# Five written-out instruction orders replaced, in a fused fp32 decoder layer

## The chip, the core and the metric

The kernel runs on one core of one Trainium2 chip. The metric is the device time of one launch in microseconds (us). Of each program several executions are timed, and one more is recorded by the hardware profiler; "the profiled execution" is that one.

## The reference

One layer of a hybrid decoder on 2048 prompt tokens and 8 single decode tokens, width 1024, in fp32:

```
xn  = rmsnorm(x);  z = xn @ w_in            # 1024 -> 1792: conv branch, gate branch, q, k, v
rec = RG-LRU(causal_conv4(xr)) * gelu(gr)   # a per-token scan, 512 channels
att = banded attention, 8 heads of 64, 2 kv heads, window 128, learned sinks
h   = x + concat(rmsnorm(rec), rmsnorm(att)) @ w_out
y   = h + (silu(rmsnorm(h) @ w_gate) * (rmsnorm(h) @ w_up)) @ w_down     # 2816 wide
out = rmsnorm(y)                            # and the last k/v rows, conv and scan states
```

The decode tokens use given caches of k, v, conv input and scan state.

## The kernel before

**Products.** Channels lie on the 128 partitions, tokens along the free axis. Each fp32 product is three matmuls of a reduced fp32 form (fp32r): both operands are split into a high part and a low rest, and hi·hi, hi·lo and lo·hi are accumulated in PSUM. So each weight tile is loaded raw, cast on ACT (`split_raw`, L936) and its rest formed on POOL (L937); each activation is cast on ACT and its rest formed on DVE or POOL (L998/L999).

**First half, to about 660 us.** The tokens go through in four tiles of 520, 512, 512 and 512. For each tile: norm; the in-projection in 14 units of 128 outputs (`ip0_9_1` is tile 0, unit 9, second half of the columns), each 24 matmuls per accumulator; conv and scan; attention block by block; the norms of the two groups; the out-projection in 8 units (`op2_5_0` is tile 2, unit 5), 24 matmuls each; the residual sum (L1638, and L1686/L1687 for the last tile) and its store to `hs` (for the last tile on ACT's queue, L1688). An attention block has scores `s`, a mask and a scale on DVE (L1515, L1526), transposes `pt`, a cast `pth` of them on ACT (L1536) and the rest `ptl` on DVE (L1537), and the product `o` with v. `pt14_1_0` is block 14, kv group 1, first part. The tiles of weights in tile 0 are loaded raw (`raw_in0_9_0`, L931), split, and stored split to DRAM (L955); tiles 1 to 3 load the split form.

**Second half, the FFN.** The tokens go in three pairs of column halves (344+344, 342+342, 342+342), and for each pair over 11 pairs of hidden blocks. For gate and up (`g`, `u`), two column halves by two hidden blocks are formed by seven products instead of eight (Strassen's scheme in Winograd's form, `w_g2_0_6`: pair 2, block pair 0, product 6); their sums of weights are made in the first token pair and kept in DRAM (`split_g`, `split_u`), and loaded later (L1802); raw blocks come by L1790 (`ru`, `rg`). `mixed` in DRAM holds the sums of the normed activations; `n0_3_1` (L1082, L1090) is such a sum on its way there, `hn` (L1137 to L1139) its load and split. Down (`pd`, L2021; `pw` with 14 rounds, L2050) is plain in some block pairs and has seven products in others. A last norm ends the kernel.

**PSUM.** Accumulators of the projections come from a pool of three banks (`ps_acc`); `ps_s` has two, `ps_t`, `ps_o` and `ps_m` one each. A tile of a pool becomes free when the operation that evicts it has ended.

**What sets the order.** Each part of the work is a generator with planned times. What an engine executes, though, is fixed by `ORDER`, a dictionary of five strings, for PE (12043 instructions), DVE (2566), ACT (1815), POOL (795) and SP (1416, each a DMA issue). A string is a list of runs `name:n`: the next n instructions of the part named so. `order` and `order_engines` walk each string and tie each instruction to the one ahead of it:

```
for run in runs.split():
    key, _, at = run.partition("+")
    key, _, n = key.partition(":")
    for _ in range(int(n or 1)):
        r = todo[key].pop(int(at or 0))
        if last is not None:
            tc.add_manual_dep(r, last.name, no_sync, reason="issue order")
        last = r
```

Each engine works through its own string in order. What it must wait for from other engines comes from the data and the buffers. A DMA that stands on SP or ACT is issued when the queue reaches it.

Of the kernel before, what the change touches and what calls it, by code (L numbers as in the profile page):

```python
# [117 lines left out]
vt0_2 ip0_13_0:13 ip0_13_1:6 vt0_3 ip0_13_1:16 ip0_2_0 ip0_13_1 ip0_2_0 ip0_13_1 ip0_2_0:4 s0_0_0:2 ip0_2_0:2 s0_0_0
ip0_2_0 s0_0_0 s0_0_1 ip0_2_0:3 s0_0_1:2 ip0_2_0:3 g0_0_0_0 ip0_2_0:4 s0_0_1 ip0_2_0:4 ip0_2_1:4 s0_1_0 ip0_2_0
ip0_2_1 s0_1_1 s0_1_0:3 ip0_2_1:2 s0_1_1:3 ip0_2_1:2 g0_0_0_260 ip0_2_1:10 s1_0_0 ip0_2_1 s1_0_0:2 ip0_2_1:2 s1_0_0  # L120
ip0_2_1 pt0_0_1 ip0_2_1 pt0_0_1:3 ip0_5_0:2 s1_0_1:2 ip0_5_0:2 s1_0_1:2 ip0_5_0:4 g0_0_1_0 ip0_5_0:10 o0_0_0 ip0_5_0:6
s1_1_0 ip0_5_1:2 s1_1_0:3 ip0_5_1:6 g0_0_1_260 ip0_5_1:3 pt0_1_1:3 ip0_5_1:3 pt0_1_1 o0_0_0 ip0_5_1:2 s1_1_1 ip0_5_1:4
s1_1_1 ip0_5_1 s1_1_1:2 ip0_5_1 ip0_4_0 ip0_5_1:2 ip0_4_0:3 s2_0_0:2 ip0_4_0 s2_0_0 ip0_4_0 s2_0_0 ip0_4_0:4 o0_1_0
ip0_4_0:6 o0_1_0 pt1_0_0 ip0_4_0 pt1_0_0 ip0_4_0:2 pt1_0_0 ip0_4_0:2 pt1_0_0 s2_0_1:4 ip0_4_0 ip0_4_1:2 ip0_4_0
ip0_4_1:6 ip0_4_0 ip0_4_1:16 ip1_8_0:12 ip0_6_0 ip1_8_0:3 ip0_6_0:5 o1_0_0 ip0_6_0:4 pt1_0_1:2 ip0_6_0 ip1_8_0 pt1_0_1
ip0_6_0 o1_0_0 pt1_0_1 g0_3_0_0 ip0_6_0:12 ip0_6_1 ip1_8_0 ip0_6_1:8 ip1_8_0 ip0_6_1:3 s2_1_0 ip0_6_1:3 s2_1_0 ip1_8_0
ip0_6_1 s2_1_0:2 ip0_6_1:4 s2_1_1 ip0_6_1:3 s2_1_1:2 o1_0_1 ip0_6_1 s2_1_1 g0_3_0_260 ip1_8_0:2 pt1_1_0 ip1_8_0
pt1_1_0:2 ip1_8_0 pt1_1_0 ip1_8_0 ip1_9_0:2 o1_0_1 ip1_9_0:9 g0_3_1_0 ip1_9_0:7 ip0_7_0:2 ip1_9_0 ip0_7_0:3 ip1_9_0
ip0_7_0:4 ip1_9_0:3 pt1_1_1:2 o1_1_0 ip1_9_0 ip0_7_0 pt1_1_1:2 o1_1_0 ip0_7_0:4 g0_3_1_260 ip0_7_0:7 s3_0_0 ip0_7_0:3
# [2130 lines left out]
```

## Time and profile before

| | |
|---|---|
| runs | 2035.62 us median of 3 (2033.41, 2041.63, 2035.62) |
| profiled execution | 2035.2 us |
| its span | 2033.4 us |
| mean granted TensorE clock | 0.995 of full speed |
| DMA | 450.98 MB, mean 222 GB/s |

The span runs from the first to the last recorded instruction; the execution's own time has 1.8 us more around it. A line of the timeline gives start, duration, engine, code line, operation, output and inputs by the program's names, the count, and in brackets how long the engine had been idle and what it waited for. PE is TensorE's matmul, PEld its weight load, DVE VectorE, ACT ScalarE, POOL GpSimd, SPq and ACTq the DMA issues of SyncE and ScalarE.

### The profile page before, as it was taken

How to read it: one execution, taken by the hardware profiler on the slowest of the kernel's cores; microseconds unless marked ns; L12 is line 12 of the kernel's file. 1: busy time of each engine (PE TensorE's matmuls, PEld its weight loads, DVE VectorE, ACT ScalarE, POOL GpSimd, SP SyncE). 2: the span in 40 equal slices, each digit the busy share in tenths (PEclk: the TensorE clock that was granted, in tenths of full speed). 3: DMA queues.
4: the chain of work that ended last, by engine and by line, in shares of the span. 5: the costliest groups of instructions: out<-in, count | busy, mean ns of one | idle time of the engine just before them, and what ended most of it. 6: DMA issues, size and time to landing. Idle time of an engine off the chain costs nothing.

```text
span 2033.4 us, 34750 instructions
## 1 busy us (share of the span) xinstructions
PE 2004.7 (99%) x12273; PEld 1904.5 (94%) x12273; DVE 1472.9 (72%) x2694; ACT 955.0 (47%) x1960; POOL 906.8 (45%) x799
## 2 busy tenths in 40 slices
PE   9999999999999999999999999999999999999997
PEld 8988887888778999999999999999999999999997
DVE  6888986777886777765555777787767666776675
ACT  5776764654563543443344533343335433433443
POOL 4312451120132796676666645565557422322333
PEclk9999999999999999999999999999999999999999
DMA  9863675667688776764546687776668675555552
GB/s 338 297 215 127 225 273 182 210 197 223 206 288 272 285 245 208 240 212 168 184 172 224 229 282 242 261 240 214 228 209 290 204 236 196 182 197 199 195 173 101
DMA packets 208991, 450.98 MB, mean 222 GB/s; under 512 B 25232, under 2 KB 82720, under 8 KB 208800
## 3 DMA queue, kind: packets, MB, share of 16 engines
q1 hardware_dynamic: 205184, 445.73, 65.2%
q10 hardware_dynamic: 3632, 3.02, 0.5%
q8 instruction: 97, 1.59, 0.3%
q14 instruction: 78, 0.64, 0.1%
HBM read 335.89 MB, written 113.84 MB: 221 GB/s over the span
## 4 chain that ended last, share of the span: by engine, by line
PE 88%; DMA 6%; DVE 4%; issue 1%; ACT 1%; SPq 0%; DVEq 0%; ACTq 0%
PE ps_g L963 20%; PE ps_u L963 20%; PE ip L963 14%; PE pw L963 12%; PE pd L963 11%; PE op L963 5%; PE s L963 1%; DMA m<-mixed 1%; PE g L963 1%; PE pt L968 1%; PE o L963 1%; DMA mixed<-n 1%; DMA y<-hs 1%; DMA xs<-in_xT 0%; DMA hn<-mixed 0%
## 5 line engine op out<-in xcount | busy, mean ns | idle before, releaser
L963 PE MATMUL ps_g<-hn,w_g 128*128 128x342 f32 (+1 forms) x2772 | 546.0, 320 | 1.8 <-DMA w_g<-split_g 1.0
L963 PE MATMUL ps_u<-hn,w_u 128*128 128x342 f32 (+1 forms) x2772 | 529.8, 320 | 4.5 <-ACT c_u L1985 3.5
L963 PEld LDWEIGHTS ps_u<-hn,w_u 128*128 128x128 f32 x2772 | 455.0, 189 | 5.5 <-ACT c_u L1985 3.8
L963 PEld LDWEIGHTS ps_g<-hn,w_g 128*128 128x128 f32 x2772 | 456.6, 189 | 2.5 <-ACT w_d L1778 2.3
L963 PE MATMUL ip<-xn,w_in 128*128 128x512 f32 (+1 forms) x1680 | 367.3, 361 | 3.9 <-ACT w_in L936 2.7
L963 PEld LDWEIGHTS ip<-xn,w_in 128*128 128x128 f32 x1680 | 271.5, 190 | 49.4 <-issue 4.8
L2050 DVE TENSOR_TENSOR y<-y,pw 128x342 f32<-128x342 f32 x504 | 242.7, 506 | 94.8 <-PE pw L963 90.4
L963 PE MATMUL pd<-fh,w_d 128*128 128x344 f32 (+1 forms) x960 | 235.0, 320 | 0.0
L963 PE MATMUL op<-mix,w_out 128*128 128x512 f32 (+1 forms) x960 | 209.8, 362 | 0.3 <-DVE mix L999 0.3
L2021 DVE TENSOR_TENSOR y<-y,pd 128x344 f32<-128x344 f32 (+1 forms) x240 | 119.6, 509 | 103.3 <-PE pd L963 91.1
L963 PEld LDWEIGHTS op<-mix,w_out 128*128 128x128 f32 x960 | 157.6, 190 | 30.0 <-issue 6.1
L963 PE MATMUL pw<-fh,wd 128*128 128x342 f32 x576 | 167.5, 319 | 1.0 <-DVE y L2021 1.0
L963 PEld LDWEIGHTS pd<-fh,w_d 128*128 128x128 f32 x960 | 167.3, 188 | 0.0
L963 PE MATMUL pw<-t,wd 128*128 128x342 f32 x648 | 150.6, 319 | 0.0
L963 PE MATMUL pd<-fl,w_d 128*128 128x344 f32 (+1 forms) x480 | 147.6, 320 | 0.0
L1946 POOL TENSOR_TENSOR c_u<-c_u,c_g 128x342 f32<-128x342 f32 (+1 forms) x60 | 58.8, 980 | 180.2 <-DVE c_u L1964 144.5
L1964 DVE TENSOR_TENSOR c_u<-c_u,ps_u 128x342 f32<-128x342 f32 (+1 forms) x99 | 50.5, 510 | 122.1 <-PE ps_u L963 121.8
L1935 DVE TENSOR_TENSOR fl<-c_u,fh 128x342 fp32r<-128x342 f32 (+1 forms) x132 | 118.5, 909 | 15.3 <-ACT fh L1934 14.2
L1779 POOL TENSOR_TENSOR w_u<-ru,w_u 128x512 fp32r<-128x512 f32 x44 | 58.9, 1340 | 151.8 <-ACT w_u L1778 123.0
L1934 ACT CAST fh<-c_u 128x342 fp32r<-128x342 f32 (+1 forms) x132 | 62.1, 479 | 106.4 <-POOL c_u L1946 41.9
L963 PEld LDWEIGHTS pw<-t,wd 128*128 128x128 f32 x648 | 111.4, 189 | 0.0
L963 PEld LDWEIGHTS pw<-fh,wd 128*128 128x128 f32 x576 | 105.6, 189 | 1.3 <-DVE y L2021 1.3
(299 smaller groups left out, 3499.9 us busy)
## 6 DMA issues: line engine op xcount, KB each, us to landing
w_g<-split_g SPq DMA_DIRECT2D x88, 512.0 KB, 4.4
w_u<-split_u SPq DMA_DIRECT2D x88, 512.0 KB, 5.5
w_in<-split_w SPq DMA_DIRECT2D x84, 512.0 KB, 3.6
rg<-in_wgate SPq DMA_DIRECT2D x110, 256.0 KB, 3.1
ru<-in_wup SPq DMA_DIRECT2D x110, 256.0 KB, 3.3
w_out<-split_w SPq DMA_DIRECT2D x48, 512.0 KB, 4.8
split_g<-w_g SPq DMA_DIRECT2D x44, 512.0 KB, 2.8
split_u<-w_u SPq DMA_DIRECT2D x44, 512.0 KB, 2.9
```

The source lines that it names most:

```text
L963: r = nc.tensor.matmul(*args, **kw)
L968: r = nc.tensor.transpose(*args)
L1779: lo_eng.tensor_tensor(w[:, 1, :], src, w[:, 0, :].bitcast(F32), op=ALU.subtract)
L1934: nc.scalar.copy(hi, v)
L1935: nc.vector.tensor_tensor(lo, v, hi.bitcast(F32), ALU.subtract)
L1946: (nc.vector if p == NPAIR - 1 or src is not v else eng(E_MUL[2 * h + n])).tensor_tensor(v, src, g, op=ALU.mult)
L1964: nc.vector.tensor_tensor(o, a, b, op)
L2021: nc.vector.tensor_tensor(ys[gi, n, m], ys[gi, n, m], ps, ALU.add)
L2050: nc.vector.tensor_tensor(v, v, ps, ALU.add)
```

## The change

The five strings of `ORDER` are replaced. All other code is the same, and each string holds the same instructions as before, in another order. The PE string has 11089 runs instead of 4667, DVE 2094 instead of 1968, ACT 1492 instead of 1476, POOL 629 instead of 624, SP 1152 instead of 1127. On PE the median instruction stands 0.79 us of matmul work away from its old place, 95% less than 3.3 us, the farthest 26.6 us. As the strings are longer, all code behind them has line numbers 406 higher (L1537 becomes L1943). One place of the PE string, around the out-projection of tile 2 and attention block 14:

```
-op2_5_0:10 s15_1_0:3 op2_5_0:2 s15_1_1 op2_5_0 s15_1_1 s15_1_0 s15_1_1:2 o14_0_1 op2_5_0:4 o14_0_1 op2_5_0:6
-pt14_1_0:3 op2_5_0 op2_6_0 pt14_1_0 op2_6_0:22 op2_7_0 op2_6_0 op2_7_0:5 st_rc3 pt14_1_1:4 op2_7_0:5 o14_1_0 op2_7_0:3
...
+op2_5_0 op2_6_0 op2_5_0 op2_6_0 op2_5_0 op2_6_0 op2_5_0 op2_6_0 op2_5_0 op2_7_0 op2_5_0 op2_7_0 op2_5_0 op2_7_0
+op2_5_0:3 op2_6_0 op2_7_0 op2_6_0 op2_7_0 op2_6_0 op2_7_0 op2_6_0 pt14_1_1 op2_6_0 pt14_1_1 op2_6_0 pt14_1_1 op2_6_0
```

Three places on other engines follow. The first is SP, the loads at the start of the kernel. Here `raw_in0_u_i` is a raw half of unit u's weights of the in-projection, `xs0` a part of the x tile, `xt1` rows of the next tile, `cs`, `scv`, `gw` and `sh` constants and states, `split_w` the store of split weights, `out_skw` and `out_svw` copies of the k and v caches to outputs. Before:

```order
L1239 DMA cs_101<-in_cst 128x384
L1185 DMA gw_132<-in_gatew 128x1024
L1184 DMA scv_137<-in_sconv 128x96
L931 DMA raw_in0_12_1_185<-in_win 128x512
L955 DMA split_w_117<-w_in0_1_0_166 128x1024
L1186 DMA sh_138<-in_sh0 128x32
L931 DMA raw_in0_9_0_368<-in_win 128x512
L955 DMA split_w_117<-w_in0_12_0_171 128x1024
L1292 DMA xt1_0_1418<-in_xR 128x512
L1292 DMA xt1_1_1421<-in_xR 128x512
L1178 DMA out_skw<-in_ck 8x16256
L1179 DMA out_svw<-in_cv 8x16256
```

The next row there is `raw_in0_9_1`. After:

```order
L1655 DMA xs0_188<-in_xT 128x520
L1337 DMA raw_in0_12_1_185<-in_win 128x512
L1655 DMA xs0_188<-in_xT 128x520
L1337 DMA raw_in0_9_0_368<-in_win 128x512
L1590 DMA scv_137<-in_sconv 128x96
L1361 DMA split_w_117<-w_in0_12_0_171 128x1024
L1698 DMA xt1_0_1418<-in_xR 128x512
L1361 DMA split_w_117<-w_in0_1_0_166 128x1024
L1698 DMA xt1_1_1421<-in_xR 128x512
L1337 DMA raw_in0_9_1_374<-in_win 128x512
L1645 DMA cs_101<-in_cst 128x384
```

`raw_in0_12_1` and `raw_in0_9_0` stand among the x parts now, `raw_in0_9_1` ahead of `cs`; `out_skw`, `sh`, `gw` and `out_svw` stand later, in this order, with other loads between them.

The second is DVE, near the end of the first half (588 to 597 us in the profile before): the scan of tile 3 (`q23_1`, `rrec`), the scale of the probabilities of block 15 (`sc15`), the residual of tile 2 (`xres2_5`), a sum of normed activations for the FFN (`n0_3`), and the rest `ptl14_1_0` of the transposed probabilities of block 14. Before:

```order
L1376 SCALAR_TENSOR_TENSOR q23_1_5902<-ia3_3_5945,carry_135,ix3_3_5952 128x512
L1384 SCALAR_TENSOR_TENSOR rrec_144<-rrec_144,q23_1_5902 128x512 x2
L1526 TENSOR_SCALAR sc15_0_6723<-sc15_0_6723,mx15_0_6724 128x256 x2
L1638 TENSOR_TENSOR xres2_5_6137<-xres2_5_6137,op2_5_0_6188 128x512
L1082 SCALAR_TENSOR_TENSOR n0_3_1_5510<-n0_3_1_5510,vec_99,hb_0_1_5363 128x344
L1082 SCALAR_TENSOR_TENSOR n0_3_0_5513<-n0_3_0_5513,vec_99,hb_0_0_5356 128x344
L1090 TENSOR_TENSOR n0_3_1_5510<-n0_3_1_5510,n0_3_0_5513 128x344
L1537 TENSOR_TENSOR ptl14_1_0_6701<-pt14_1_0_6695,pth14_1_0_6700 128x512
```

After:

```order
L1782 SCALAR_TENSOR_TENSOR q23_1_5902<-ia3_3_5945,carry_135,ix3_3_5952 128x512
L1943 TENSOR_TENSOR ptl14_1_0_6701<-pt14_1_0_6695,pth14_1_0_6700 128x512
L1790 SCALAR_TENSOR_TENSOR rrec_144<-rrec_144,q23_1_5902 128x512
L1955 TENSOR_TENSOR ratt_145<-o14_0_6659,ratt_145 64x4x128
L2044 TENSOR_TENSOR xres2_5_6137<-xres2_5_6137,op2_5_0_6188 128x512
L1488 SCALAR_TENSOR_TENSOR n0_3_1_5510<-n0_3_1_5510,vec_99,hb_0_1_5363 128x344
L1488 SCALAR_TENSOR_TENSOR n0_3_0_5513<-n0_3_0_5513,vec_99,hb_0_0_5356 128x344
L1496 TENSOR_TENSOR n0_3_1_5510<-n0_3_1_5510,n0_3_0_5513 128x344
L1932 TENSOR_SCALAR sc15_0_6723<-sc15_0_6723,mx15_0_6724 128x256 x2
```

`ptl14_1_0` moved from behind the `n0_3` rows to right behind the scan, and the scale of block 15 moved behind them.

The third is SP at the start of the last token pair (about 1555 us): `hn2_*` are loads of its activations, `y2_0` loads from `hs`, `rg` and `ru` raw weight blocks, `w_g2_0_6` the gate weights of product 6. Before:

```order
L1790 DMA ru2_0_00_17775<-in_wup 128x512
L1137 DMA hn2_0_6_17545<-mixed_113 128x342
L1790 DMA rg2_1_00_17912<-in_wgate 128x512
L1137 DMA hn2_0_7_17549<-mixed_113 128x342 x2
L1790 DMA rg2_0_11_17805<-in_wgate 128x512
L1137 DMA hn2_1_0_17572<-mixed_113 128x342
L1137 DMA hn2_1_1_17576<-mixed_113 128x342 x2
L1774 DMA y2_0_18171<-hs_112 128x342 x2
L1802 DMA w_g2_0_6_17543<-split_g_114 128x1024
```

After:

```order
L1543 DMA hn2_0_7_17549<-mixed_113 128x342
L2196 DMA rg2_1_00_17912<-in_wgate 128x512
L2180 DMA y2_0_18171<-hs_112 128x342
L1543 DMA hn2_1_0_17572<-mixed_113 128x342
L1543 DMA hn2_0_7_17549<-mixed_113 128x342
L1543 DMA hn2_1_1_17576<-mixed_113 128x342
L2208 DMA w_g2_0_6_17543<-split_g_114 128x1024
L2180 DMA y2_0_18171<-hs_112 128x342
L1543 DMA hn2_1_2_17599<-mixed_113 128x342
L2196 DMA ru2_0_00_17775<-in_wup 128x512
L1543 DMA hn2_1_1_17576<-mixed_113 128x342
```

`w_g2_0_6` stands ahead of one of the two `y2_0` loads, of `ru2_0_00` and of the second `hn2_1_1` load now.

Three more moves: on PE the matmuls that use the gate weights `w_g1_0_6` (about 1112 us) and `w_g2_0_6` (about 1562 us) stand seven FFN matmuls later among the others; on DVE the operation for `fl1_4_01` (L1935, about 1330 us) stands 17 rows earlier; on ACT the load of an activation table (L1943, about 672 us) stands five rows earlier among its neighbours, the store of `xres3_4` to `hs` (L1688, about 674 us) behind it one row earlier, and the copy `c_u0_0_10` (L1985, about 680 us) still behind both.

More of the change, by code (lines that the diff above doesn't have):

```diff
@@ new lines @@
+op0_5_260 op0_6_0 op0_5_260 op0_6_260 op0_5_260 op0_6_260 op0_5_260 op0_6_0 op0_5_260 op0_6_0 op0_5_260 op0_6_0
+op0_5_260 g1_3_1_0 op0_5_260 op0_6_0 op0_6_260 op0_6_0 o6_0_0 op0_6_0 op0_5_260 op0_6_0 pt6_0_1 op0_6_0 pt6_0_1
+op0_6_0 op0_5_260 bc_x2_0 op0_6_0 op0_6_260 op0_6_0 pt6_0_1 op0_6_0 op0_6_260 op0_6_0 pt6_0_1 op0_6_0 op0_6_260
+op0_6_0 op0_6_260 op0_6_0 o6_0_0 op0_6_260 op0_7_0 op0_6_260 op0_7_0 op0_6_260 op0_7_0 op0_6_0 op0_6_260 op0_7_0
+op0_6_260 s7_1_0 op0_6_260 op0_6_0 op0_6_260 pt6_1_0 op0_6_260 o6_0_1 s7_1_0 op0_6_260 o6_0_1 op0_6_260 s7_1_0
@@ new lines @@
+d2_10_1_1 d2_10_2_1 d2_10_4_1 d2_10_2_1 d2_10_3_1 d2_10_2_1 d2_10_3_1 d2_10_4_1 d2_10_3_1 d2_10_4_1 d2_10_3_1
+d2_10_5_1 d2_10_6_1 d2_10_3_1 d2_10_6_1 d2_10_3_1 d2_10_5_1 d2_10_4_1 d2_10_7_1 d2_10_6_1 d2_10_5_1 d2_10_4_1
+d2_10_7_1 d2_10_5_1 d2_10_7_1 d2_10_5_1 d2_10_7_1 d2_10_5_1 d2_10_6_1 d2_10_7_1 d2_10_6_1 d2_10_7_1 d2_10_6_1
+d2_10_0_0 d2_10_2_0 d2_10_0_0 d2_10_2_0 d2_10_0_0 d2_10_1_0 d2_10_0_0 d2_10_3_0 d2_10_0_0:2 d2_10_1_0 d2_10_2_0
+d2_10_1_0:4 d2_10_2_0 d2_10_3_0 st_f2_1:3 d2_10_2_0 d2_10_3_0 d2_10_5_0 d2_10_3_0 d2_10_6_0 d2_10_5_0 d2_10_3_0
@@ L572 @@
[L572 to L574 removed]
+pre pre+2 pre+3 pre+3 pre+1 pre+1 pre pro+3 pro pro+2 pro pro+15 pro:5 x0:6 x0+1 x0+2 x0+3 x0+4 x0:5 pro:3 r01+3 r01+4
+x0 pro:6 r01 q02 r01 pro:2 pro+1 pro k0 v0+1 v0 q02 r01:2 k0 r01 k0 r00:2 k0+2 k0+1 k0 k1+1 k1+1 r03:2 r01+1 q01 r01
@@ L686 @@
+pu2.6:3 wd2.6 wg2.7 wd2.6 wu2.7 pu2.7:2 wd2.7 pu2.7:3 wd2.7 wg2.8 wd2.7 wu2.8 pu2.8:2 wd2.8 pu2.8:3 wd2.8 wg2.9 wd2.8
+wu2.9 pu2.9:2 wd2.9 pu2.9:3 wd2.9 wg2.10 wd2.9 wd2.10 wu2.10 wd2.10 wd2.10+1 wd2.10 f21:3 f20:8
 """,
     "SP": """
-x0:9 x0+1 x0+1 x0+1 pro+1 pro x0 r01 pro v0 q02 xs1:2 cache:2 v0+1 r01 k0 q02 k0+1 v0 r00 v0 xs1:2 r00+1 k0 r03 k0
-r03+1 r00 xs1:2 q01 r00 q01+1 r03 q00 r03 xs1:2 q00+1 q01 q03 q01 q03+1 x1 q00 x1 r02 q00 r02+1 q03 x1 g01 q03 x1
-g01+1 r02 g00 r02 x1:2 g00+1 g01:2 g02 x1 g00 k1 g02+1 g03 x1 k1 g00 g02 g03+1 xs2 v1 g02 v1 xs2:2 o00 cache g03 o00+1
@@ L741 @@
[L741 to L745 removed]
+x0+1 x0:4 x0+2 x0 x0+1 x0 x0+1 x0:2 v0 pro q02 xs1 r01 xs1 v0+1 x0 k0 r01 xs1 v0 k0+1 r00 q02 r00+1 xs1 cache pro+1 k0
@@ new lines @@
+r03 v0 r03+1 xs1 pro k0 q01 r00+1 xs1 q01+1 r00 r03 q00 xs1:2 q00+1 cache q03 q01 r03 x1 q03+1 x1 q01 r02 q00:2 r02+1
+x1 g01 x1 q03:2 r02 g01+1 x1 g00 r02 x1 g00+1 g01 x1 g02 g01 g00 g02+1 x1 k1 g03 k1 xs2 g00 g02 g03+1 v1 g02 o00 v1
+xs2:2 cache g03 o00+1 q10 g03 o01 q10 q11 xs2 dec:2 q11 g10 xs2:3 g10 r10:2 xs2 o00+2 x2 q12:2 q13 x2 q13 r11:2 g11:2
+r12:2 g12:2 r13 o01+3 r13 g13:2 o01+1 o00 o02 o00 o02+1 o01 o03 o01 o03+1 o02 x2:2 o02 o04 o00 x2 o04+1 o03 o02 x2 o01
+o05 o03 x2 o03 x2 o02 o05+1 o04+2 o04 o06 o04 o06+1 o05 o03 o07 o05:2 o07+1 o06 o04 o06 wg0.0 o06 g20 o07 wg0.0 o07
@@ L746 @@
+wg2.9 wu2.8+4 wd2.8 wg2.9 wu2.8 wd2.8:3 wu2.8 wd2.8 wu2.8:2 wg2.9+4 wu2.9 wg2.9 wd2.8 wg2.9 wd2.8 wg2.9 wu2.9 wg2.9
+wd2.8 wg2.10 wu2.9+4 wd2.9 wg2.10 wd2.9+1 wu2.9 wd2.9:3 wu2.9:3 wu2.10 wg2.10+4 wg2.10 wd2.9 wg2.10 wd2.9 wg2.10:2
+wu2.10 wd2.9 wd2.10:2 wu2.10+4 wd2.10:2 wu2.10:4 f21:8 f20:4
 """,
```

1640 lines of the change are left out of this document (1013 added, 627 removed).

## The prediction

> **What bounds the kernel now.** I read the page first, then the busy time by stretches of the span, then the single instructions around each hole on TensorE.
>
> ```profile
> span 2033.4 us, 34750 instructions
> PE 2004.7 (99%) x12273; PEld 1904.5 (94%) x12273; DVE 1472.9 (72%) x2694; ACT 955.0 (47%) x1960; POOL 906.8 (45%) x799
> PE 88%; DMA 6%; DVE 4%; issue 1%; ACT 1%; SPq 0%; DVEq 0%; ACTq 0%
> ```
>
> TensorE is busy for 99% of the span, and the chain that ended last is TensorE for 88% of it. So order can win only where TensorE stands idle or runs at a lowered clock. The stretches show where; the columns are the stretch, its length, the busy time of PE, PEld, DVE, ACT and POOL with their counts, the granted clock, the DMA share and GB/s.
>
> ```profile
> 0.00:27.00 27.00, 22.09 (x149) 21.16 (x150) 15.77 (x33) 16.47 (x30) 10.22 (x16) 0.94 0.90 332
> 27.00:584.00 557.00, 556.17 (x3167) 473.40 (x3167) 453.31 (x968) 351.62 (x745) 143.84 (x162) 1.00 0.68 224
> 584.00:621.00 37.00, 32.27 (x151) 25.98 (x150) 29.21 (x57) 18.34 (x42) 12.53 (x11) 0.91 0.71 233
> 621.00:660.00 39.00, 38.74 (x183) 31.70 (x183) 24.58 (x37) 14.03 (x29) 12.43 (x9) 1.00 0.94 318
> 660.00:685.00 25.00, 21.35 (x119) 20.25 (x118) 18.33 (x27) 13.12 (x27) 16.44 (x13) 0.93 1.02 376
> 685.00:1203.00 518.00, 515.37 (x3289) 514.30 (x3288) 342.66 (x503) 217.29 (x433) 345.28 (x264) 1.00 0.63 215
> 1203.00:1564.00 361.00, 359.58 (x2286) 359.03 (x2285) 272.61 (x473) 142.37 (x288) 212.05 (x193) 1.00 0.71 237
> 1564.00:2010.00 446.00, 446.00 (x2848) 445.94 (x2847) 303.58 (x575) 173.76 (x354) 145.79 (x127) 1.00 0.59 195
> 2010.00:2033.40 23.40, 13.08 (x95) 12.71 (x93) 12.81 (x28) 8.00 (x16) 8.26 (x9) 0.83 0.36 121
> 605.71:609.12 3.41, 2.34 (x14) 1.73 (x14) 3.41 (x5) 1.67 (x4) 1.27 (x1) 1.00 0.94 296
> 609.12:615.95 6.83, 5.64 (x17) 4.39 (x17) 6.25 (x13) 4.10 (x8) 1.52 (x1) 0.50 0.53 156
> 677.39:680.80 3.41, 0.35 (x2) 0.35 (x3) 0.44 (x2) 0.84 (x3) 2.36 (x2) 1.00 1.04 409
> 680.80:684.21 3.41, 3.41 (x14) 3.41 (x13) 0.94 (x2) 2.15 (x5) 1.70 (x2) 0.50 1.04 413
> ```
>
> Length less PE busy gives the idle time: 4.91 at the start, 0.83, 4.73, 0.26, 3.65, 2.63, 1.42, 0.00, and 10.32 in the end, 28.75 us in all. The last four rows are windows inside the others. Two of them show a granted clock of 0.50, and of the 5.64 and 3.41 us that TensorE was busy in these, half is lost: 2.8 and 1.7 us. The rest is TensorE at its cadence, where the same multiset of instructions must take the same time, unless interleaving itself costs something.
>
> **The change part by part.** *Interleaved accumulators.* Where TensorE worked 10 or 24 matmuls on one accumulator, it now changes accumulator at almost every matmul. The trace has both forms in one place.
>
> ```profile
> 1107.94 3.45 PE L963 MATMUL ps_u<-hn,w_u 128*128 128x344 f32 x21
> 1112.16 0.55 PE L963 MATMUL ps_g<-hn,w_g 128*128 128x342 f32 x2 [0.78 <-ACT w_d L1778]
> 1112.56 0.32 PE L963 MATMUL ps_u<-hn,w_u 128*128 128x344 f32 x1
> 1112.71 0.32 PE L963 MATMUL ps_g<-hn,w_g 128*128 128x342 f32 x1
> ```
>
> Twenty-one in a row take 3.45 us, 0.156 us from start to start after taking off one 0.32 for the last one's length; alternating starts are 0.15 to 0.16 apart (1112.56, 1112.71). I cost the interleaving at nothing. The bounds are a hundredth of a microsecond either way, read off these starts.
>
> *Start.* SyncE issues its loads one after the other, and two matmul groups of the first token tile wait on weights.
>
> ```profile
> 14.26 0.83 SPq L1178 DMA_DIRECT2D out_skw<-in_ck  x1
> 15.15 0.67 SPq L1179 DMA_DIRECT2D out_svw<-in_cv  x1
> 15.93 0.37 SPq L931 DMA_DIRECT2D raw_in<-in_win  x1
> 24.58 0.62 ACT L936 CAST w_in<-raw_in 128x512 fp32r<-128x512 f32 x1 [2.76 <-DMA raw_in<-in_win]
> 15.29 8.32 PE L963 MATMUL ip<-xn,w_in 128*128 128x260 f32 x67 [0.44 <-ACT w_in L936]
> 25.25 0.62 PE L963 MATMUL ip<-xn,w_in 128*128 128x260 f32 x3 [1.65 <-ACT w_in L936]
> ```
>
> The raw half behind the second wait (raw_in0_9_1) is issued at 15.93 and its cast starts at 24.58, idle 2.76 us for that landing. Before it on SyncE stood the constants, gw, sh and both cache copies; now these come later, and raw_in0_12_1 and raw_in0_9_0 move ahead too. With the two cache issues alone gone it goes out 0.83+0.67 = 1.5 us sooner, and by their shapes 1.8 MB less lies ahead of it in a stretch that moves 332 GB/s. I take both waits as gone: 0.44+1.65 = **2.1 us**. Bounds: 0, if landings in this full stretch don't follow the order of issue, and 2.1. What moves back is needed later: gw feeds the gates, the cache copies feed outputs only. The first 6 us (first x tile and first weights) I leave as they are.
>
> *588 to 597.* One transpose group waits on VectorE.
>
> ```profile
> 590.75 0.68 DVE L1638 TENSOR_TENSOR xres<-xres,op 128x512 f32<-128x512 f32 x1
> 593.72 1.74 DVE L1082 SCALAR_TENSOR_TENSOR n<-n,vec,hb 128x344 f32<-128x344 f32 x2 [2.30 <-DMA n<-hs]
> 595.93 0.68 DVE L1537 TENSOR_TENSOR ptl<-pt,pth 128x512 fp32r<-128x512 f32 x1
> 596.67 0.66 PE L968 MATMUL pt<-cs,sc 128*128 128x128 f32 x4 [2.11 <-DVE ptl L1537]
> 587.74 0.59 ACT L1536 CAST pth<-pt 128x512 fp32r<-128x512 f32 x1 [1.04 <-PE pt L968]
> ```
>
> The ptl operation (ptl14_1_0) needs only the pth that ACT ended at 588.33, but stands behind n0_3_1, whose load from hs lands at 593.7. VectorE idles 2.30 us and TensorE then 2.11. The new table puts ptl14_1_0 ahead of that row and of the others shown, right behind the scan. I take the 2.11 as won: **2.1 us**; nothing else of TensorE hangs on n0_3_1 for some 60 us. The chain pt15 after it (further ptl waits up to 615, with half clock) keeps its length between its members, so I leave it: 0, with the stretch's other 4.73−2.11 = 2.6 idle and 2.8 of clock as the far end.
>
> *680.* The largest single wait.
>
> ```profile
> 673.86 0.35 ACTq L1688 DMA_DIRECT2D hs<-xres  x1
> 679.96 0.45 ACT L1985 COPY c_u<-ps_u 128x344 f32<-128x344 f32 x1 [4.18 <-DMA m<-mixed]
> 680.45 1.25 PE L963 MATMUL ps_u<-hn,w_u 128*128 128x344 f32 x4 [3.55 <-ACT c_u L1985]
> ```
>
> The copy writes memory that the store of 673.86 still reads, and transfers of 376 GB/s fill this stretch. In the new ACT table this store is issued a few rows earlier; the copy still follows it by the same rule. I take **0.5 us** of 3.55; bounds 0 and 3.55+1.7 of half clock, which goes if the wait goes.
>
> *FFN.* Four waits, 1112.16 above (0.78) and these:
>
> ```profile
> 1183.28 0.71 PE L963 MATMUL ps_u<-hn,w_u 128*128 128x342 f32 x3 [0.82 <-DMA w_u<-split_u]
> 1199.19 0.42 PE L963 MATMUL pw<-fh,wd 128*128 128x342 f32 x1 [1.04 <-DVE y L2021]
> 1330.23 0.43 PE L963 MATMUL pw<-fl,wd 128*128 128x342 f32 x1 [0.38 <-DVE fl L1935]
> 1562.22 0.40 PE L963 MATMUL ps_g<-hn,w_g 128*128 128x342 f32 x1 [1.04 <-DMA w_g<-split_g]
> ```
>
> At 1112 and 1562 the waiting product now stands seven FFN matmuls, about 1.1 us, later, and at 1562 the load w_g2_0_6 also goes out ahead of a half of y2_0 and of ru2_0_00. At 1330 the fl operation moves 17 VectorE rows forward. Those three go: 0.78+1.04+0.38 = **2.2 us**. The waits of 1183 and 1199 keep their neighbours; I leave them. The end after 2010 (10.32 idle) is a serial norm, unchanged.
>
> *New waits.* A finer order also brings some consumers nearer to their producers. I counted sixteen on TensorE whose new place lies 0.3 to 1.6 us ahead of the time at which before's trace had their data; most producers move forward with them. As no such wait exists in before, its nearest rows are the FFN waits of 0.38 to 1.04: I charge one of the longer, **−1.0 us**; the bounds are none and all sixteen, 0 to 16.
>
> Sum: 2.1+2.1+0.5+2.2−1.0 = 5.9. The profiled execution took 2035.2 us, 1.8 outside its span, and lies 0.4 under the median of the runs, 2035.62: 2035.2−5.9 = **2029.3 us**.
>
> **The rivals.** *Nearly every hole closes.* If landings and durations are absorbed throughout, the idle time outside the first 27 us and the end goes (28.75−4.91−10.32 = 13.5), with the start's 2.1 and the clock's 4.5: 20.1 us, 2015. Against it stands the fixed order of the 680 store and of pt15; for it, that each of these waits hangs on one row. Short of all, 2015 to 2025.
>
> Whether the clock comes back is told by the rows of 677: busy for 0.35 of 3.41 us, and half clock in the next 3.41. The Trainium skill ("TensorE: Matmul & The Clock Gate", Part 1, section "What's actually happening") puts the gate's fall at an idle window of about 3.4 us; this row agrees. The window from 605.71, busy for 2.34 of 3.41, should by that rule not have been followed by half clock, but the next row shows 0.50; so the trace agrees only in part. By the rule alone that half clock would not be owed to short waits, and this rival's gain would lack its 2.8.
>
> *Nothing changes.* Landings at 332 to 376 GB/s and the serial chains decide: the start and 680 stay, what FFN gives is eaten by new waits. 2033 to 2038.
>
> *Slower: three accumulators open at once.*
>
> ```profile
> L963 PE MATMUL ip<-xn,w_in 128*128 128x512 f32 (+1 forms) x1680 | 367.3, 361 | 3.9 <-ACT w_in L936 2.7
> L963 PE MATMUL op<-mix,w_out 128*128 128x512 f32 (+1 forms) x960 | 209.8, 362 | 0.3 <-DVE mix L999 0.3
> ```
>
> These are 1680/24 = 70 and 960/24 = 40 groups over a pool of three banks. Interleaved, neighbours end close together and three banks must be evicted at once, each by a VectorE operation of 0.68 us (590.75). If one group in four waits for one: 27×0.68 = 18.4 us, less the gains of 6.9: 2046.7; two more half-clock windows of 1.7 each: 2050. I put it at 2046 to 2056; it decides from some 25 of the 110 groups on. Against it: both rows have almost no idle time now (4.2 us together, nearly all at the start), and VectorE is busy 453 of 557 us there. The Trainium skill (the same page, section "A second HAM failure mode: psum-queue depth-cycling") tells of TensorE idling briefly between groups when PSUM banks are cycled, until the clock swings; the alternating matmuls at 1112 ran 0.15 apart in a stretch at clock 1.00, so here the rule is not borne out.
>
> **How the numbers follow.** Forecast (2025.4 to 2033) 0.44; most holes close (2015 to 2025) 0.33; no change (2033 to 2038) 0.13; slower (2046 to 2056) 0.10. A measurement of this kernel can tell about 0.5%, 10 us, from no change, so faster means under 2025.4, slower over 2045.8: 0.33, 0.57, 0.10. The range leaves out the slower case and the last microsecond of the second, and reaches past the third by some of the sixteen new waits: 2016 to 2041.
>
> **What would show it.** Right: no wait on w_in casts at 15 and 25; no wait of 2 us before a pt transpose near 597; 680 with about 3 us left; the waits of 1112, 1330 and 1562 gone, 1183 and 1199 still there; PE busy still about 2004. Wrong: half clock gone near 610 and 680 (then the second case); waits of ip or op on a VectorE eviction (then the slower one); matmul starts over 0.16 apart in the interleaved FFN.

## The result, and the profile after

| | before | after |
|---|---|---|
| median of 5 runs each | 2036.14 us (2033.41 to 2041.63) | 2066.26 us (2063.79 to 2069.47) |
| profiled execution, its span | 2035.2, 2033.4 us | 2069.47, 2067.7 us |
| granted clock | 0.995 | 0.995 |

The ratio is 1.0145, 95% interval 1.0125 to 1.0165: the new orders cost 30 us. The forecast was 2029.3 in a range of 2016 to 2041, so it is wrong in sign and outside its range.

First the head of the page of after; the code lines of after stand 406 further down than before's (L963 is L1369 now).

```profile
span 2067.7 us, 34791 instructions
PE 2029.2 (98%) x12273; PEld 1896.6 (92%) x12273; DVE 1455.4 (70%) x2694; ACT 948.4 (46%) x1960; POOL 910.1 (44%) x799
```

The span grew by 34.3 us, but TensorE's idle time only from 28.7 to 38.5. Its *busy* time grew by 24.5, with the same 12273 matmuls at the same clock. A matmul is recorded for about 0.32 us though the next starts 0.157 later. So a start that is late by less than the difference leaves no idle time in the record; it only thins out the matmuls. Counts show that. After by the same stretches as in the prediction:

```profile
0.00:27.00 27.00, 23.13 (x168) 21.98 (x169) 20.74 (x43) 16.91 (x32) 15.96 (x18) 1.00 0.90 311
27.00:584.00 557.00, 550.12 (x3099) 461.29 (x3099) 437.02 (x938) 340.26 (x729) 139.84 (x159) 1.00 0.66 220
584.00:621.00 37.00, 33.01 (x163) 25.24 (x163) 34.81 (x66) 23.09 (x46) 12.98 (x13) 0.99 0.85 269
621.00:660.00 39.00, 38.69 (x166) 31.48 (x167) 17.96 (x32) 11.61 (x23) 6.16 (x5) 0.92 0.79 261
660.00:685.00 25.00, 24.75 (x134) 21.52 (x133) 23.28 (x33) 15.17 (x31) 16.01 (x11) 1.00 0.94 321
685.00:1203.00 518.00, 510.92 (x3209) 500.50 (x3208) 325.99 (x491) 214.42 (x434) 342.42 (x262) 1.00 0.63 213
1203.00:1564.00 361.00, 358.30 (x2249) 351.97 (x2248) 262.48 (x462) 132.19 (x267) 205.36 (x185) 1.00 0.70 231
1564.00:2010.00 446.00, 443.63 (x2801) 437.49 (x2801) 297.22 (x562) 175.42 (x362) 153.10 (x132) 1.00 0.63 207
```

Add up the first count of each row. Before had started 3316 matmuls by 584 us, after 3267: 49 behind. At 685 it is 39 behind, at 1203 119, at 1564 156, at 2010 203. At 0.157 us each, 203 are 32 us. So most is lost in the FFN, a little in every stretch and at full clock, and part of it in the first 584 us; from 584 to 685, where the waits of 597 and 680 had been, after catches up.

Cadence is unharmed. Two accumulators in turn, in after's timeline:

```profile
1355.77 0.32 PE L1369 MATMUL ps_g<-hn,w_g 128*128 128x342 f32 x1
1355.93 0.32 PE L1369 MATMUL pw<-fh,wd 128*128 128x342 f32 x1
1356.09 0.32 PE L1369 MATMUL ps_g<-hn,w_g 128*128 128x342 f32 x1
```

Starts lie 0.16 apart, and over some 8400 pairs in the FFN the median is 157.0 ns in both traces. What is new are waits. After's waits of TensorE (us in total, times, longest):

```profile
PE pt L1374 <- DVE ptl L1943: 4.0, 6, 1.4
PE pd L1369 <- DVE y L2427: 3.2, 6, 0.9
PE pw L1369 <- DVE y L2456: 2.8, 7, 0.9
PE ps_g L1369 <- DVE c_g L2370: 1.6, 3, 0.6
```

`y<-y,pd`, `y<-y,pw` and `c_g` are the VectorE operations that read a finished accumulator and so free its PSUM bank; `ptl` is the last to read the transposes `pt`, whose pool has one bank. Before had one such wait in the FFN (1.04 us). This view counts idle time alone. I therefore also compared each matmul's start with the usual distance for its pair of shapes, and counted those over 40 ns late (worked out from the traces):

| starts over 40 ns late: number, us | before | after |
|---|---|---|
| within 150 ns behind the end of a VectorE operation that frees the bank | 7, 6.7 | 68, 26.2 |
| the same behind a VectorE operation that makes an operand | 5, 3.7 | 20, 7.4 |
| the same behind ACT or POOL | 9, 9.7 | 17, 8.6 |
| behind no wait | 376, 45.7 | 617, 64.8 |
| all (with second passes of split matmuls) | 66.1 us | 109.4 us |

The difference of 43 us is more than the 34.3 of the span: the usual distance is taken for each pair of shapes, and after has other pairs, so this is a size and no balance. The starts directly behind a wait cost 22 us more, and those behind VectorE 23 us more: this growth is VectorE's alone. The starts behind no wait cost another 19 us more. In the FFN of after, 63 of 68 matmuls that started late behind a wait are followed by one that is late too, by 106 ns in the median and 6.6 us in all; for the rest of the 19 us no cause is shown.

One of the late starts behind VectorE, from the timeline of after:

```profile
896.75 2.98 POOL L2185 TENSOR_TENSOR w_u<-s_u,w_u 128x512 fp32r<-128x512 f32 x2 [3.39 <-ACT w_u L2184]
896.77 1.83 DVE L2185 TENSOR_TENSOR w_u<-s_u,w_u 128x512 fp32r<-128x512 f32 x1
898.52 0.92 DVE L2427 TENSOR_TENSOR y<-y,pd 128x344 f32<-128x344 f32 x2
897.92 0.32 PE L1369 MATMUL ps_u<-hn,w_u 128*128 128x344 f32 x1
899.07 0.91 PE L1369 MATMUL pd<-fh,w_d 128*128 128x344 f32 x4 [0.84 <-DVE y L2427]
```

A subtraction of 128x512 on VectorE took 1.83 us; GpSimd had started one of its own 20 ns earlier. The eviction behind it came late, and the matmul that wanted its bank waited 0.84 us. The same at 936 us:

```profile
933.46 1.44 DVE L2185 TENSOR_TENSOR w_u<-ru,w_u 128x512 fp32r<-128x512 f32 x1
934.29 1.75 POOL L2219 TENSOR_TENSOR s_g<-rg,rg 128x512 f32<-128x512 f32 x1
934.82 1.60 DVE L1496 TENSOR_TENSOR n<-n,n 128x342 f32<-128x342 f32 x1
936.34 0.50 DVE L2427 TENSOR_TENSOR y<-y,pd 128x344 f32<-128x344 f32 x1
936.89 0.42 PE L1369 MATMUL pd<-fh,w_d 128*128 128x344 f32 x1 [0.95 <-DVE y L2427]
```

The mean of a group hides this. The groups by form (busy us, mean ns), an eviction and an operation with both inputs in SBUF, of before:

```profile
L2050 DVE TENSOR_TENSOR y<-y,pw 128x342 f32<-128x342 f32 x504 | 242.7, 506 | 94.8 <-PE pw L963 90.4
L1935 DVE TENSOR_TENSOR fl<-c_u,fh 128x342 fp32r<-128x342 f32 x88 | 68.2, 785 | 11.7 <-ACT fh L1934 11.4
```

Same shape, 506 against 785 ns. One by one, those with both inputs in SBUF take 0.51 us while GpSimd is still, and up to 1.66 while it works (once 2.26); those that read PSUM take 0.49 to 0.52 either way. In before 330 VectorE operations are held by more than 100 ns, 238.6 us in all; in after 330, 233.8 us. So the holding isn't new. What is new is that TensorE stands right behind it: of after's 88 late starts behind VectorE, 56 (27.3 us) have a held operation in the unbroken run of VectorE ahead of them; in before 6 of 12 (2.2 us).

### The profile page after: what moved, and what is told of

Read it like the earlier page. It is cut to its first block, busy times and chain, and to the rows that moved or that the text cites. A ratio compares the mean times of both kernels' runs of the same rounds, so it can differ in the third digit from the quotient of the medians.

```text
span 2067.7 us, 34791 instructions
## 1 busy us (share of the span) xinstructions
PE 2029.2 (98%) x12273; PEld 1896.6 (92%) x12273; DVE 1455.4 (70%) x2694; ACT 948.4 (46%) x1960; POOL 910.1 (44%) x799
## 5 line engine op out<-in xcount | busy, mean ns | idle before, releaser
L1369 PE MATMUL ps_g<-hn,w_g 128*128 128x342 f32 (+1 forms) x2772 | 732.6, 322 | 3.9 <-DVE c_g L2370 1.6
L1369 PE MATMUL ps_u<-hn,w_u 128*128 128x342 f32 (+1 forms) x2772 | 676.5, 320 | 0.5 <-DVE c_g L2370 0.5
L1369 PEld LDWEIGHTS ps_g<-hn,w_g 128*128 128x128 f32 x2772 | 491.7, 188 | 11.2 <-DVE c_g L2370 2.0
L1369 PEld LDWEIGHTS ps_u<-hn,w_u 128*128 128x128 f32 x2772 | 481.7, 188 | 4.4 <-DVE c_u L2370 1.4
L1369 PE MATMUL ip<-xn,w_in 128*128 128x512 f32 (+1 forms) x1680 | 395.5, 365 | 3.0 <-DVE xn L1405 1.6
L1369 PEld LDWEIGHTS ip<-xn,w_in 128*128 128x128 f32 x1680 | 270.8, 189 | 47.2 <-issue 4.1
L1369 PE MATMUL pd<-fh,w_d 128*128 128x344 f32 (+1 forms) x960 | 245.4, 322 | 3.7 <-DVE y L2427 3.2
L1369 PE MATMUL op<-mix,w_out 128*128 128x512 f32 (+1 forms) x960 | 234.9, 369 | 1.6 <-DVE xres L2044 1.2
L1369 PE MATMUL pw<-t,wd 128*128 128x342 f32 x648 | 195.8, 321 | 1.6 <-DVE y L2456 1.3
L1369 PEld LDWEIGHTS op<-mix,w_out 128*128 128x128 f32 x960 | 161.9, 192 | 31.9 <-issue 5.3
L1369 PE MATMUL pw<-fh,wd 128*128 128x342 f32 x576 | 177.4, 322 | 1.8 <-DVE y L2456 1.5
L1369 PEld LDWEIGHTS pd<-fh,w_d 128*128 128x128 f32 x960 | 168.3, 188 | 8.4 <-DVE y L2427 5.7
L1369 PE MATMUL pd<-fl,w_d 128*128 128x344 f32 (+1 forms) x480 | 137.9, 320 | 0.6 <-DVE fl L2341 0.5
L1369 PEld LDWEIGHTS pw<-t,wd 128*128 128x128 f32 x648 | 120.0, 189 | 4.7 <-DVE y L2456 3.0
L1369 PEld LDWEIGHTS pw<-fh,wd 128*128 128x128 f32 x576 | 107.1, 189 | 4.4 <-DVE y L2456 1.6
```

Of the source, the lines that this page charges most:

```text
L1369: r = nc.tensor.matmul(*args, **kw)
```

## The experiments

My theory after the result: **the new order of TensorE has no room.** It puts matmuls right behind the VectorE operations that free their bank or make their operand, and these come late when GpSimd holds VectorE. In before 15 matmuls start within 0.15 us of the end of the last VectorE operation that they need, and 30 within half a microsecond; in after 146 and 378. The rivals: interleaving costs by itself; banks are reused too soon whatever VectorE does (other matmuls between the last one of an accumulator and the first of the next in its bank: median 40 in before, 24 in after; fewer than nine, which is 1.4 us at 0.157 us each, in 10 of 1029 cases before and 168 after); another engine's order is at fault.

**Which half.** The orders of all five engines spliced: after's up to 672 us and before's behind it, and the reverse (splice at 664).

```
 first half   0 .. 672 us: after's five orders     then before's
 second half  0 .. 664 us: before's five orders    then after's
```

> All five new orders up to 672 us of their own execution, then the old orders for what is left, so the FFN runs in the old order. Theory (everywhere, the new order lets TensorE follow VectorE's operations too closely, so that each late one is a stall): about half of the 30 us of loss, 2050 us, bounds 2045 to 2056. Rival named in the prediction (only the three-bank pool of the in- and out-projection is short): the whole loss, 2062 to 2068. Rival (the loss sits in the FFN): 2030 to 2038.

> The old orders up to 664 us, then the new ones, so only the FFN is interleaved. Theory: the other half, 2052 us, bounds 2046 to 2058. Rival of the three-bank pool: 2034 to 2038. Rival that the loss sits in the FFN: 2062 to 2068.

The first took 2044.38 us, 1.0035 of before (1.0021 to 1.0049); the second 2054.24, 1.0085 (1.0063 to 1.0106). So both halves lose, 7.6 us and 17.5, the FFN more. The first lies just under the theory's 2045 to 2056, the second within its 2046 to 2058; both lie outside the rivals' ranges. Together they are 25 of the 30 us; the 5 us that are left are within the noise of the three measurements.

**GpSimd's long operations shortened.** In both kernels each two-dimensional subtraction of 256 columns or more on GpSimd becomes a memset of the same tile. This leaves out the rests of those split operands; instructions, orders and dependencies stay.

```
+whole = nc.gpsimd.tensor_tensor
+def part(o, a, b, op):
+    if op == ALU.subtract and len(o.shape) == 2 and o.shape[1] >= 256:
+        return nc.gpsimd.memset(o.bitcast(F32), 0.0)
+    return whole(o, a, b, op=op)
+nc.gpsimd.tensor_tensor = part
```

> Before, with GpSimd's subtractions on two-dimensional tiles of 256 or more columns replaced by a write of zeros to the same tile: the rests of split operands are zero, so that part of the computation is left out. Theory (VectorE's operations with two SBUF operands are held up by a running GpSimd operation, up to 1.1 us each, and the old order has room for it): little change, 2025 to 2036 us. Rival (switching accumulators costs TensorE itself): 2025 to 2036 too; it speaks only of the next run.

> After, with the same replacement, the same part left out. Theory: VectorE's SBUF operations are no longer held up, most short waits on VectorE go, and half or more of the 30 us of loss with them: at most 2045 us. Rival (the interleaving itself costs TensorE): as slow as after, 2058 us or more.

Before became 2030.73 us, 0.9972 (0.9961 to 0.9982); after became 2037.42, 0.9999 of before (0.9987 to 1.0011). So the same edit gives before 6 us and after 29, and the gap between the two orders shrinks from 30 us to 6.7. From after so shortened:

```profile
L2464 DVE TENSOR_TENSOR y<-y,pw 128x342 f32<-128x342 f32 x504 | 239.8, 506 | 108.5 <-PE pw L1377 105.4
L2349 DVE TENSOR_TENSOR fl<-c_u,fh 128x342 fp32r<-128x342 f32 x88 | 49.1, 562 | 13.0 <-ACT fh L2348 12.0
```

The evictions themselves are as fast as ever, 506 ns; the operations ahead of them are mostly no longer held (562 ns; 114 held in place of 330), and late starts behind a bank fall from 26.2 to 12.8 us. Of 308 VectorE additions, subtractions and products that ran beside one of the memsets alone, none was held; the held ones that are left ran beside GpSimd operations that read. The edit also makes GpSimd's results come sooner, so it doesn't separate the two by itself; but only 3 late starts of after (2.6 us) were behind GpSimd's own results.

**TensorE's order alone.** In after, only PE's table is written anew: a list of the same instructions in which each keeps its dependencies and is placed by the longer of its durations in the two profiled executions. 815 of 12043 instructions move; the other four tables are after's. At the place of 899 us, the rows of PE in after from the last matmul of accumulator `pd_4_3_1` to the first of `pd_4_6_0`, which takes its bank:

```order
L1369 MATMUL pd_4_3_1_10082<-fh_4_11_7187,w_d_4_10_9941 128x344
L1369 MATMUL pd_4_4_0_10093<-fl_4_10_7190,w_d_4_11_10018 128x344
L1369 MATMUL pd_4_4_1_10101<-fh_4_11_7187,w_d_4_11_10018 128x344
L1369 MATMUL pd_4_4_0_10093<-fh_4_10_7186,w_d_4_11_10018 128x344
L1369 MATMUL pd_4_4_1_10101<-fl_4_11_7191,w_d_4_11_10018 128x344
L1369 MATMUL pd_4_5_0_10121<-fl_4_00_7188,w_d_4_01_9974 128x344
L1369 MATMUL ps_u_5_1_10192<-hn_0_0_6179,w_u_5_1_10071 128x344
L1369 MATMUL pd_4_6_0_10145<-fh_4_00_7184,w_d_4_01_9974 128x344
```

The same in the new list; eleven rows are left out, of `pd_4_4_0`, `pd_4_4_1`, `pd_4_5_0`, `pd_4_5_1` and `ps_u`:

```order
L1306 MATMUL pd_4_3_1_10082<-fh_4_11_7187,w_d_4_10_9941 128x344
L1306 MATMUL pd_4_4_0_10093<-fl_4_10_7190,w_d_4_11_10018 128x344
...
L1306 MATMUL pd_4_5_0_10121<-fh_4_10_7186,w_d_4_11_10018 128x344
L1306 MATMUL pd_4_6_0_10145<-fh_4_00_7184,w_d_4_01_9974 128x344
```

Thirteen matmuls stand between the two now, six before. The interleaving stays: PE's string has 10136 runs, against 11089 in after and 4667 in before.

> After, with only TensorE's order changed: 815 of its 12043 instructions stand later or earlier, so that none stands ahead of data that either of the two traces delivers later (for each operation the longer of its two durations); it stays interleaved, 10136 runs, and the other four orders are those of after. Theory (consumers follow too closely): most of the 30 us come back, 2040 us, bounds 2030 to 2050. Rival (the other four orders are late whatever TensorE does): 2058 us or more. Rival (interleaving costs TensorE itself): 2058 or more.

Measured 2037.22 us, 1.0009 of before (0.9998 to 1.002): 29 of the 30 us come back. The same place in its timeline:

```profile
885.62 3.00 POOL L2122 TENSOR_TENSOR w_u<-s_u,w_u 128x512 fp32r<-128x512 f32 x2 [2.42 <-ACT w_u L2121]
885.65 1.82 DVE L2122 TENSOR_TENSOR w_u<-s_u,w_u 128x512 fp32r<-128x512 f32 x1
887.38 1.86 DVE L2364 TENSOR_TENSOR y<-y,pd 128x344 f32<-128x344 f32 x4
887.43 0.32 PE L1306 MATMUL ps_u<-hn,w_u 128*128 128x344 f32 x1
887.90 0.47 PE L1306 MATMUL pd<-fh,w_d 128*128 128x344 f32 x2
```

VectorE is held just as long, 1.82 us, and TensorE doesn't wait: other matmuls fill the time. Over the run 336 operations are held (239.9 us), but only 15 late starts are behind a bank (4.3 us) and 6 behind a VectorE operand (1.5). So neither interleaving nor the other four orders is the cause by itself.

**A floor under the reuse of banks.** In after, PE's table alone, with first matmuls moved back until no bank is taken again within 1.5 us of matmul work. This lengthens one kind of distance and leaves the operands' as it was. (The 152 of 628 of the expectation are a selection; of all 1029 cases 168 have fewer than nine matmuls between in after, and 39 here.)

> After, with TensorE's order changed for one kind of distance only: from the last matmul of a PSUM accumulator to the first one of the next accumulator in the same bank there is never less than 1.5 us of matmul work (152 of 628 were under it); the other four orders are those of after. Theory (both kinds of distance count, banks and operands, and a held-up VectorE operation takes up to 1.1 us longer): a part of the loss comes back, the stalls of those 152 in the trace of after with what follows them, about 12 us: 2054 us, bounds 2046 to 2060. Rival (bank reuse alone makes the loss): 2036 to 2042 us. Rival (banks have no part in it): 2064 us or more.

It took 2070.99 us, 1.0168 (1.0154 to 1.0182): no better than after. The theory's 2046 to 2060 is missed, the rival that bank reuse alone makes the loss falls, and the one that gives banks no part (2064 or more) has the number. From its waits:

```profile
PE pd L1348 <- DVE y L2406: 2.8, 6, 0.9
PE pw L1348 <- DVE y L2435: 2.3, 5, 1.1
```

The waits on evictions are still there: 54 late starts behind a bank, 21.9 us, against 68 and 26.2, and those behind ACT for operands rose from 3.8 to 8.4 us: a first matmul that moves back lets others move forward. So the run doesn't isolate the distance, and a larger floor wasn't run. It does show that short distances as such don't make the loss, for the new list of PE, the one that gave 29 us back, still has 130 cases with fewer than nine matmuls between. Nor did that list lengthen the distance to VectorE everywhere (551 matmuls start within 1 us of the VectorE operation that they need; after has 599, before 59). It thinned out the closest ones: 61 start within 0.15 us, in after 146 and with the floor 116.

**The same list pass on before.** 122 instructions of PE move.

> Before, with TensorE's order changed by the same rule: 122 instructions moved, 4623 runs. Theory: the old order had room nearly everywhere, so little is to be won, 2030 to 2036 us. Rival (the waits come from transfers and no order helps): 2036 us.

2034.47 us, 0.9994 (0.9984 to 1.0003): nothing measurable. Before had the room already.

**The gains by themselves.** Before with after's orders up to 28 us only; and with these and after's once more from 656 to 677 us, which holds the store and the copy of the wait at 680.

> All five new orders up to 28 us of their own execution, then the old ones. The term of the prediction for the start: 2.1 us won, 2034.5 us. Rival (landings decide): 2036.5 us.

> As the run before, and the new orders once more from 656 us of the old execution to 677 us of the new one, around the largest single wait of before (3.55 us and half clock behind it, in the trace of after gone). Theory: 2.1 and up to 5.3 us won, 2029 to 2033 us. Rival (the wait hangs on what stood ahead in the first half, and comes back): 2034 us.

The start alone: 2035.08 us, 0.9996 (0.9985 to 1.0008), 1.3 us by the medians and within the interval none; it lies between the 2034.5 of the term and the 2036.5 of its rival and decides nothing. With the piece at 656: 2030.66, 0.9977 (0.9967 to 0.9987), 5.7 us in all. The second of these by stretches:

```profile
0.00:27.00 27.00, 23.07 (x167) 21.90 (x168) 20.69 (x41) 16.95 (x32) 15.92 (x18) 1.00 0.88 311
660.00:685.00 25.00, 23.63 (x145) 22.71 (x144) 18.58 (x25) 15.45 (x32) 16.98 (x12) 1.00 1.02 378
```

From 660 to 685 us 3.65 us of idle time became 1.37, and the clock 0.93 became 1.00.

**The step at 597 alone.** Before with one row moved on DVE: `ptl14_1_0` right behind the scan step `q23_1`.

> Before, with one VectorE instruction moved: ptl14_1_0 right behind the scan of tile 3, ahead of the n0_3 rows. The term of the prediction for 588 to 597 us: the wait of 2.11 us gone, 2034.3 us. Rival (the next link of that chain waits instead): the wait ahead of the transposes near 597 gone, the time unchanged, 2036.4 us.

2036.03 us, 0.9998 (0.9989 to 1.0007). The wait of 2.11 us is gone and nothing is won; the timeline shows where the chain waits now:

```profile
600.30 0.47 PE L958 MATMUL o<-pth,vt 128*128 128x512 f32 x1 [1.09 <-DVE ratt L1544]
609.32 0.50 PE L958 MATMUL o<-pth,vt 128*128 128x512 f32 x1 [1.01 <-ACT pth L1531]
611.02 0.66 PE L963 MATMUL pt<-cs,sc 128*128 128x128 f32 x4 [1.20 <-DVE ptl L1532]
```

The first is new, the second was 0.50 us in before and the third 0.92. From 584 to 621 TensorE idles 5.04 us, where it was 4.73.

**A better order.** The kernel with the new start and the piece at 656, with 80 of PE's instructions moved by the same list pass.

> The kernel with the new start and the new stretch around 680 us, with 80 matmuls moved so that none stands ahead of data that its own trace or that of before delivers later (the longer of the two durations of each operation). Theory: a few more short waits go, 2026 to 2030 us. Rival (what is left is transfers and serial chains): 2030.7 us.

2027.24 us (2025.08 to 2031.8), 0.9954 (0.9941 to 0.9968): 9 us faster than before and 39 than after. Over the kernel with the two pieces alone it gains 3.4 us by the medians, and the two intervals just meet.

## Why the prediction was wrong

**The step that failed is the last term, "New waits … −1.0".** I "counted sixteen" consumers whose place lay ahead of the time at which before's trace had their data, and priced them by the waits that before had. The trace has 105 late starts behind another engine where before had 21; they cost 42.2 us against 20.1, and starts behind no wait cost 19 us more. The count failed, not just the price: it took the producers' times as fixed and asked who comes too early by 0.3 us or more. It should have asked how many stand with less room than a producer's spread, and 146 matmuls start within 0.15 us of theirs.

The spread was there to be read. In before's groups two operations of one shape differ, 506 and 785 ns, and I took 0.68 us from a single row for all. Each of the 330 held operations was in before's trace: 319 ran while a GpSimd operation did, and ended one own length, less 0.12 us (0.10 to 0.17 for eight in ten), after that had ended. The Trainium skill (SBUF — State Buffer, section "Who interferes with whom") says that a VectorE instruction with two SBUF inputs contends with a GpSimd instruction that reads SBUF, and not with one that only writes it. This case agrees: the evictions, which have one input in PSUM, are never held (0.49 to 0.52 us), and with GpSimd's subtractions replaced by memsets none of 308 VectorE operations beside a memset alone was held. The prediction didn't draw on it.

**"I cost the interleaving at nothing."** Right for the cadence (157.0 ns in both), and the relisted run bears it out: nearly as finely interleaved as after, and 29 us faster. But the new order also took room, as a bank is taken again after 24 other matmuls in the median and not 40, and 146 matmuls follow VectorE within 0.15 us and not 15; that I didn't price.

**"The same multiset of instructions must take the same time"** outside the idle time was a misreading. Busy time held late starts already in before (66.1 us in all, of which 28.7 are idle), so there was room to lose there that the share of 99% doesn't show.

**The start, 2.1.** Both waits on `w_in` at 15 and 25 us are gone, as said, but waits on `xn` took their place:

```profile
9.09 6.50 PE L1369 MATMUL ip<-xn,w_in 128*128 128x260 f32 x52 [0.70 <-DVE xn L1405]
17.43 5.30 PE L1369 MATMUL ip<-xn,w_in 128*128 128x260 f32 x42 [0.70 <-DVE xn L1405]
```

Idle time there fell by 1.0 us (4.91 to 3.87), and the clock rose from 0.94 to 1.00. That clock can't be credited to the order: the run with `ptl14_1_0` alone has before's start and reads 0.98 there, with its half clock mostly behind 27 us. Alone the start measured 1.3 us by the medians, which is not clear of noise.

**588 to 597, 2.1.** Wrong: the wait went, and `o` and `pt` waited elsewhere in the chain, as the run with that step alone shows. I had written that the chain of pt15 keeps its length, and drew the wrong conclusion: if it does, an earlier `ptl14` wins nothing.

**680, 0.5.** Right in sign, too small: the wait on `c_u` is gone from after's list, 660 to 685 idles 0.25 us where it was 3.65, at full clock. Added to the new start, the piece gave 4.4 us (2035.08 to 2030.66), near the far bound of 5.25. These two intervals touch. In that run the store goes out 4.1 us earlier (669.76 for 673.86), and the copy waits for nothing. One reading there was wrong: by the addresses in the built program the copy's tile (`c_u0_0_10`) and the store's (`xres3_4`) don't overlap, and why the copy waits for that store all the same is open.

**FFN, 2.2.** The matmuls that had waited at 1330 and 1562 start without a wait, those of 1183 and 1199 too, which I had left as they were. That of 1112 waits 0.35 us in place of 0.78, now for its load:

```profile
1133.18 0.55 PE L1369 MATMUL ps_g<-hn,w_g 128*128 128x342 f32 x2 [0.35 <-DMA w_g<-split_g]
```

By idle time these gave some 3.7 us, more than 2.2, though no run has them alone, and the new waits cover it many times over: 44 late starts behind a bank that VectorE frees, 14.4 us, stand in the FFN.

**The rivals.** "Slower" had the kind right, evictions by VectorE that are late for the next accumulator. It had the place wrong (the out-projection has 2 such late starts, 1.9 us; the rest lie in attention, gates and FFN) and too low a price, since it took an eviction at its unheld length: 2066 lies above its 2046 to 2056 too. Its chance of 0.10 was too small. A clock that swings while PSUM banks are cycled, as the Trainium skill ("TensorE: Matmul & The Clock Gate", section "A second HAM failure mode: psum-queue depth-cycling") tells, isn't borne out: with 44 late starts behind banks the clock stays 1.00 in the FFN. "Nearly every hole closes" was half right: holes closed, and the time was lost where none had been.

What stays open: how much of the 29 us that after gains with a shortened GpSimd comes by its earlier results and not by the holding; what makes the starts behind no wait late, beyond those right behind a wait; and whether a larger floor under the banks would have won.

## What to carry to other kernels

Before an order is tightened, take for each producer the spread of its duration, not the mean, and give its consumer that much other work: with 146 matmuls within 0.15 us of their producer the new order lost 30 us here, and moving 815 instructions of TensorE gave 29 back. Where TensorE is 98% busy, compare counts of matmuls by stretch, since waits shorter than a matmul are recorded as busy time. A wait that is removed counts only if nothing else in its chain is due at the same time; move that one row alone before summing.

## What the runs showed of the hardware

A VectorE addition, subtraction or product on two SBUF inputs of 128x342 took 0.51 us alone and up to 1.66 (once 2.26) beside GpSimd, one of 128x512 0.69 and up to 1.83; one of 128x342 or 128x344 with an input from PSUM 0.49 to 0.52 in every case. A matmul that waited costs more than its wait: in the FFN of after the next one was late as well in 63 of 68 cases, by 106 ns in the median. Half clock, too, came back elsewhere. In after the wait at 680 is gone, but two windows in the chain of block 15 read so:

```profile
616.76:620.17 3.41, 2.02 (x12) 1.14 (x10) 2.55 (x5) 2.49 (x6) 1.77 (x1) 1.00 0.93 306
620.17:627.00 6.83, 6.83 (x23) 5.77 (x23) 6.37 (x13) 4.22 (x8) 0.00 (x0) 0.50 0.84 280
```

As at 609 us in before (2.34 of 3.41 us), the clock fell behind a window in which TensorE was busy for more than half of the time (2.02 of 3.41 us) with several short waits, not behind an idle one. Of the falls in the middle of the two kernels only the one at 680.80 us of before followed a window that was nearly idle (0.35 us busy).
